# Counting a change of tile shape in the list schedule that orders a hybrid encoder's mixer

## The chip, the cores and the metric

The kernel runs on one core of one Trainium2 chip. The metric is the device time of one execution in microseconds (us). The kernel before was timed three times: 1622.95, 1623.58 and 1627.89 us, with a median of 1623.58 us. One execution was profiled; its own time is 1624.16 us, and its span from the first to the last instruction is 1622.4 us.

## The reference

Two layers work on 512 tokens of width 1024, all in float32. The change lies in the mixer of layer 0, which feeds two branches from one input projection and joins them in one output projection:

```
z   = rmsnorm(h, mix_norm) @ mix_w_in                 # 1024 -> 1792 (RWKV) + 1536 (Hyena)
y_a = rwkv7_bidir(z[..., :RWKV_COLS], ...)            # 8 heads x 64, two directions, delta-rule state
y_b = hyena_bidir(z[..., RWKV_COLS:], ...)            # gated short conv, long filter by FFT, gate
h   = h + concat([y_a, y_b]) @ mix_w_out
...
# rwkv7_bidir, one scan per direction:
sa = S kk_t ;  S = S * w_t - sa (kk_t a_t)^T + v_t k_t^T ;  y_t = S r_t
# hyena_bidir:
y = irfft(rfft(v * x1) * rfft(filter)) + (v * x1) * bias ;  y = y * x0
```

What follows in the kernel (a gated feed-forward block and a per-layer embedding in each layer, and neighbourhood attention in layer 1) is not touched by the change.

## The kernel before

The tokens lie along the free axis (512), the channels on the partitions in tiles of 128. A projection is computed as three products of rounded parts (high times high, high times low, low times high), each a TensorE matmul of 128x128 weights on 128x512 data.

`mixer0` does not write its instructions directly. `both_mixers` records every operation in a `Plan`, in groups; consecutive TensorE operations of a group are joined to a `Step` until the step's estimated cost passes 0.4. `Plan.schedule` then makes the order by list scheduling: for each engine it looks at the steps that are ready, takes those that could begin within `AHEAD` of the earliest, and of these the one of highest rank; of the five engines' candidates the earliest goes next. The rank of a step is the longest path behind it plus 1000 times the group's number in the table `ORDER`. `in_order` pins the result, so that each engine (and SP, whose queue issues all DMAs) runs its instructions in exactly that order. An instruction that waits therefore holds up all that stands behind it on its engine.

The groups, with m = 0 to 3 for four tiles of 128 channels (two heads each):

- `z,m` and `hyena,m` are input projections (72 matmuls each); `prep,m,d` makes the scan's operands for one direction d, with 64x128 products, transposes, and stores to DRAM.
- `inverse,m` inverts the triangular systems of tile m. It stores four blocks (`nd`), loads them in another layout (`w<-nd`), does 15 substitution steps on VectorE, stores and reloads (`xd`), and ends with 64x64 and 32x32 products; `kt_d` is then loaded over the inverted operand.
- `scan,m` is the recurrence over 8 chunks, each a chain of small products (64 rows or columns of the array) with copies on ScalarE and VectorE between them. `out,m` normalises its result: a product with a constant (`b<-w,con`), row sums (`b<-con,w 128x2`), a power on GpSimd, four transposes (`b<-con,w 128x128`), and the gate (`b<-sg,gup`).
- The FFT filter of Hyena: `filters` makes the filter, `fparts,j` loads it from DRAM (`w<-hw_d`), `kf,fc,j` transforms it, `signals` and `ab,fc` transform the signal (tables `wr<-in_dft_f`), `spectrum` (inside `ab`) multiplies, and `back,m` transforms back (tables `in_dft_i`, products 128x256). A table passes through a load into `wr` (3 buffers), a ScalarE rounding and a GpSimd copy into `wp`, and then a product `b<-w,wp`.
- `emb,l` projects the per-layer inputs (fills TensorE and is stored for later); `early,g` multiplies the first three finished RWKV tiles with their rows of the output weights.

In the stage's last part `scan,3`, `out,3`, `early` and `back` run; the first matmul behind the stage (line 599, tile `g`) starts at 508.26 us. All TensorE instructions recorded in a plan bear line 562 in the profile, so groups are told apart by their tiles: `b<-uv`, `b<-x,uv`, `b<-r,w` and `b<-uv,dg` are a scan, `b<-w 64x64` and `32x32` an inverse, `b<-w,wp` a transform or an embedding, `b<-xh,w` and `b<-xl,w` `early`, `b<-w 128x256` `back`.

Of the kernel before, what the change touches and what calls it, by code (L numbers as in the profile page):

```python
# [19 lines left out]
P = 128  # L20
# [184 lines left out]
class Step:  # L205

    __slots__ = ("engine", "calls", "cost", "port", "table", "bytes", "columns", "touch", "after", "then", "rank",
                 "group", "n", "left", "at", "end", "opens")

    def __init__(self, engine, group, n):  # L210
        self.engine, self.group, self.n = engine, group, n
        self.calls, self.cost, self.port, self.table, self.bytes, self.columns = [], 0.0, False, None, 0, 0
        self.touch, self.after, self.then, self.rank = {}, {}, [], 0.0
        self.opens = []


class Recorder:
# [9 lines left out]
class Plan:  # L227
# [1 line left out]

    HOP, OWN, AHEAD = 0.2, 0.1, 0.2
    DRAG, SMALL = 0.0, 5

    def __init__(self, nc):
        self.nc = nc
# [87 lines left out]
    def price(self, s, method, kw, outs, ins):  # L324

        n, e = self.width(outs[0]), s.engine
        if e == "tensor":
            rows, cols = min(P, self.rows(ins[0])), self.width(ins[0])
            if method == "transpose":
                t = n * 0.00085  # L330
            elif ins[0].dtype == F32R:
                t = 0.004 + n * 0.000447
            elif rows <= 64 or cols <= 64:
                k = (32 if rows <= 32 else 64 if rows <= 64 else P) * (32 if cols <= 32 else 64 if cols <= 64 else P)
                t = max(n * k / P / P / 500, 0.031 if cols <= 32 else 0.057)
                if cols < 4:
                    t = 0.223
            else:
                t = max(n / 600, 0.223)
            s.cost += t  # L340
            s.columns += t * 2400 * rows / P
            return
        big = sum(self.width(x) >= n for x in ins)
        if method == "memset":
            s.cost = 0.11
        elif e == "gpsimd":
            if kw.get("op") == ALU.pow:
                s.cost = 0.17 + n * 0.185
            else:
                s.cost, s.port = 0.15 + n * (0.0021 if len(ins) > 1 else 0.0009), True  # L350
        elif e == "scalar":
            s.cost = 0.16 + n * 0.00086 + 0.09 * (len(ins) - 1)
            s.table = {AF.Sin: 1, AF.Tanh: 2, AF.Exp: 2}.get(kw.get("func"))
        else:
            inner = all(x.tensor.space != PSUM for x in ins)
            if method == "tensor_reduce":
                s.cost = 0.14 + self.width(ins[0]) * 0.00105
            elif method == "tensor_tensor_scan":
                s.cost, s.port = 0.15 + n * 0.0021, True
            elif big < 2 and inner and method != "transpose":  # L360
                s.cost = 0.15 + n * 0.00053
            else:
                s.cost = 0.15 + n * 0.00106 + (0.05 if method == "scalar_tensor_tensor" else 0.0)
                s.port = inner and big > 1
# [23 lines left out]
    def schedule(self):  # L388
# [11 lines left out]
        free = dict.fromkeys(engines, 0.0)  # L400
# [3 lines left out]
        live, last, done = set(), {}, set()  # L404
# [4 lines left out]
        def key(t):  # L409
            return self.tiles[t].cap_key  # L410
# [9 lines left out]
        def start(s):  # L420

            e = s.engine
            t = max(free[e], s.at)
            want = {}
            for x in s.touch:
                if x not in live and self.pooled(x):
                    k = key(x)
                    want[k] = want.get(k, 0) + 1
            if want and (s.group not in begun or self.scarce in want):
                n = want.get(self.scarce, 0)  # L430
                g = s.group
                mine = self.reserve(g, live, [x for x in s.touch if x not in live]) if g in self.spans else 0
                rest = sum(v for h, v in reserved.items() if h != g)
                if g not in begun and not lifted and mine + n > self.SMALL:
                    n += max((self.reserve(h, live, ()) for h, r in waiting.items() if h != g and r > s.rank), default=0)
                if mine + rest + n > len(slots[self.scarce]):
                    return math.inf
            for k, n in want.items():
                have = slots[k]
                if len(have) < n:  # L440
                    return math.inf
                t = max(t, sorted(have)[n - 1])
            if s.port:
                for u, v in taken[other[e]]:
                    if u <= t < v:
                        t = v
            return t

        lifted = False
        while True:  # L450
            best = None
            waiting = {}
            for e in engines:
                for s in ready[e]:
                    g = s.group
                    if g not in begun and g in self.spans and s is self.firsts[g]:
                        waiting[g] = s.rank
            for e in engines:
                c = [(start(s), s) for s in ready[e]]
                c = [x for x in c if x[0] < math.inf]  # L460
                if not c:
                    continue
                m = max(free[e], min(x[0] for x in c)) + self.AHEAD
                t, s = max((x for x in c if x[0] <= m), key=lambda x: x[1].rank)
                if best is None or t < best[0]:
                    best = t, s
            if best is None:
                if lifted:
                    break
                lifted = True  # L470
                continue
            lifted = False
            t, s = best
            e, c = s.engine, s.cost
            ready[e].remove(s)
            if e == "tensor":
                tick = int(t / self.TICK)
                columns[tick] = columns.get(tick, 0) + s.columns
                if columns.get(tick - 1, 0) < self.COLUMNS:
                    c *= 2  # L480
            if s.table and s.table != table:
                table, c = s.table, c + 1.3
            if s.port:
                taken[e].append((t, t + c))
            free[e] = end = t + c
            if s.bytes:
                dma = max(dma, t) + s.bytes / 340e3
                end = dma + 2.1
            s.end = end
            order.append((t, s))  # L490
            g, changed = s.group, False
            for x in s.touch:
                if self.pooled(x):
                    k = key(x)
                    if x not in live:
                        live.add(x)
                        begun.add(g)
                        changed = True
                        have = slots[k]
                        have.sort()  # L500
                        have.pop(0)
                    last[x] = max(last.get(x, 0.0), end)
                    uses[x] -= 1
                    if not uses[x]:
                        slots[k].append(last[x])
                        done.add(x)
                        changed = True
            if changed and g in self.spans and g in begun:
                reserved[g] = self.reserve(g, live, (), done)
            for x in s.then:  # L510
                x.left -= 1
                x.at = max(x.at, end + (self.HOP if x.engine != e or s.bytes else self.OWN))
                if not x.left:
                    ready[x.engine].append(x)
# [50 lines left out]
class Kern:  # L565
# [186 lines left out]
    def mixer0(self):  # L752
# [17 lines left out]
        with ExitStack() as st:  # L770
# [25 lines left out]

    SLABS, PARTS = 44, 12

    ORDER = dict(start=200, low=190, filters=77, scan=100, inverse=90, prep=80, z=79, out=60, hyena=50,
                 fparts=56, kf=39, signals=62, ab=44, back=59, early=30, emb=10)  # L800

    def order(self, group):
        name, *n = group if isinstance(group, tuple) else (group,)
# [4 lines left out]
        if name in ("prep", "z"):  # L808
            n = [5 * n[0]]
        return self.ORDER[name] - (n[0] if n else 0)  # L810

# [1078 lines left out]
```

## Time and profile before

| what | value |
|---|---|
| runs | 1622.95, 1623.58, 1627.89 us (median 1623.58) |
| profiled execution: time / span | 1624.16 / 1622.4 us |
| TensorE (PE) busy over the span | 1544.8 us, 95% |
| VectorE, ScalarE, GpSimd busy | 978.7, 719.5, 325.4 us |
| stage of the mixer, until its last wait ends | 0 to 508.26 us |
| mean granted TensorE clock | 0.976 |

In the views, PE is TensorE, PEld its weight loads, DVE VectorE, ACT ScalarE, POOL GpSimd, SP (or SPq) the engine that issues DMAs. A row of windows gives, for a stretch of the span, its length, each engine's busy time in us with its number of instructions, the granted TensorE clock as a share of full speed, the DMA share and GB/s. A row of the timeline gives start, length, engine, line, operation, tiles, for a matmul the tile shape (rows by columns of the array), the count, and in brackets the idle time before it with what ended it. A float32 product shows as two matmul records, one of rounded parts and a transpose as one. A row of the chain gives start, length and what the end of the kernel waited for at that time.

### The profile page before, as it was taken

How to read it: one execution, taken by the hardware profiler on the slowest of the kernel's cores; microseconds unless marked ns; L12 is line 12 of the kernel's file. 1: busy time of each engine (PE TensorE's matmuls, PEld its weight loads, DVE VectorE, ACT ScalarE, POOL GpSimd, SP SyncE). 2: the span in 40 equal slices, each digit the busy share in tenths (PEclk: the TensorE clock that was granted, in tenths of full speed). 3: DMA queues.
4: the chain of work that ended last, by engine and by line, in shares of the span. 5: the costliest groups of instructions: out<-in, count | busy, mean ns of one | idle time of the engine just before them, and what ended most of it. 6: DMA issues, size and time to landing. Idle time of an engine off the chain costs nothing.

```text
span 1622.4 us, 24675 instructions
## 1 busy us (share of the span) xinstructions
PE 1544.8 (95%) x9576; PEld 1227.8 (76%) x9576; DVE 978.7 (60%) x1609; ACT 719.5 (44%) x1206; POOL 325.4 (20%) x286
## 2 busy tenths in 40 slices
PE   8999999996886999999999999999999999999998
PEld 6767777764565888888888878778778888888886
DVE  2587585865553766624774664565675665366654
ACT  4553635663432544413443563655554443144332
POOL 3574445533240300000001322011030000000020
PEclk9999999997987999999999999999999999999999
DMA  6366456677454233232324232323112322222421
GB/s 215 96 190 181 133 154 177 214 220 215 145 179 141 100 100 104 91 101 95 95 100 144 90 130 91 111 81 126 61 65 92 104 93 102 91 87 95 166 94 65
DMA packets 116310, 200.16 MB, mean 123 GB/s; under 512 B 27729, under 2 KB 57297, under 8 KB 116194
## 3 DMA queue, kind: packets, MB, share of 16 engines
q1 hardware_dynamic: 116194, 198.59, 38.3%
q8 instruction: 75, 1.23, 0.3%
q14 instruction: 41, 0.34, 0.1%
HBM read 166.04 MB, written 30.93 MB: 121 GB/s over the span
## 4 chain that ended last, share of the span: by engine, by line
PE 85%; DMA 4%; DVE 4%; ACT 2%; SPq 2%; POOL 1%; issue 1%; DVEq 0%; POOLq 0%; ACTq 0%
PE g L599 62%; PE b L562 19%; DVE w L562 3%; SPq L562 2%; PE m L599 1%; PE s L599 1%; DMA wr<-in_dft_f 1%; PE m L1835 1%; POOL w L562 1%; DMA wr<-in_dft_i 1%; ACT w L562 1%; ACT oh L613 0%; DMA pj_d<-w 0%; DMA wr<-in_mix_w_in 0%; DVE ol L605 0%
## 5 line engine op out<-in xcount | busy, mean ns | idle before, releaser
L605 DVE TENSOR_TENSOR wlo<-wraw,whi 128x1024 fp32r<-128x1024 f32 x186 | 235.5, 1268 | 325.8 <-ACT whi L613 321.0
L613 ACT CAST whi<-wraw 128x1024 fp32r<-128x1024 f32 x186 | 193.5, 1041 | 424.4 <-PE g L599 408.1
L599 PE MATMUL g<-xh,whi 128*128 128x512 f32 x872 | 342.0, 392 | 13.2 <-ACT whi L613 13.2
L599 PE MATMUL g<-xh,wlo 128*128 128x512 f32 x872 | 340.6, 391 | 0.0
L599 PE MATMUL g<-xl,whi 128*128 128x512 f32 x872 | 340.3, 390 | 0.0
L599 PEld LDWEIGHTS g<-xh,whi 128*128 128x128 f32 x872 | 164.4, 188 | 48.5 <-ACT whi L613 13.4
L599 PEld LDWEIGHTS g<-xh,wlo 128*128 128x128 f32 x872 | 164.2, 188 | 35.3 <-DVE wlo L605 0.8
L599 PEld LDWEIGHTS g<-xl,whi 128*128 128x128 f32 x872 | 164.3, 188 | 33.9
L605 POOL TENSOR_TENSOR nacc<-nsq 128x512 f32<-128x512 f32 x5 | 9.2, 1833 | 777.3 <-PE g L599 639.7
L562 PE MATMUL b<-xh,wp 128*128 128x512 f32 x416 | 142.2, 416 | 9.1 <-ACT wp L562 9.1
L599 PE MATMUL g<-hh,whi 128*128 128x512 f32 x352 | 137.2, 390 | 0.0
L599 PE MATMUL g<-hh,wlo 128*128 128x512 f32 x352 | 137.0, 389 | 0.0
L599 PE MATMUL g<-hl,whi 128*128 128x512 f32 x352 | 137.0, 389 | 0.0
L602 DVE SCALAR_TENSOR_TENSOR c<-u,prm,c 128x511 f32<-128x511 f32 x176 | 126.5, 747 | 6.4 <-ACT c L608 5.9
L562 PEld LDWEIGHTS b<-xh,wp 128*128 128x128 f32 x416 | 77.8, 192 | 32.6 <-ACT wp L562 10.5
L608 ACT ACTIVATE c<-u,prm 128x512 f32<-128x512 f32 x88 | 70.3, 816 | 70.8 <-DVE u L605 70.8
L562 POOL TENSOR_TENSOR wp<-wr,wp 128x512 fp32r<-128x512 f32 x60 | 80.1, 1350 | 64.9 <-ACT wp L562 30.2
L562 PE MATMUL b<-w 64*64 64x128 f32 (+5 forms) x1692 | 84.3, 253 | 7.3 <-POOL w L562 3.5
L562 POOL TENSOR_TENSOR w<-w 128x256 f32<-128x256 f32 (+2 forms) x72 | 76.6, 1083 | 68.0 <-ACT w L562 41.4
L562 PE MATMUL b<-xl,wp 128*128 128x512 f32 x208 | 85.2, 417 | 0.0
L562 PEld LDWEIGHTS b<-w 64*64 64x64 f32 (+4 forms) x1692 | 62.9, 136 | 26.5 <-issue 9.2
L605 DVE TENSOR_TENSOR u<-g,rstd 128x512 f32<-128x512 f32 x104 | 71.4, 687 | 16.5 <-PE g L599 15.6
(170 smaller groups left out, 2563.4 us busy)
## 6 DMA issues: line engine op xcount, KB each, us to landing
wraw<-in_up SPq DMA_DIRECT2D x88, 512.0 KB, 3.4
wraw<-in_down SPq DMA_DIRECT2D x44, 512.0 KB, 3.5
wr<-in_mix_w_in SPq DMA_DIRECT2D x52, 256.0 KB, 2.9
wraw<-in_na_w_qkv SPq DMA_DIRECT2D x24, 512.0 KB, 3.5
x<-ch_d SPq DMA_DIRECT2D x16, 640.0 KB, 7.2
ch_d<-w SPq DMA_DIRECT2D x64, 128.0 KB, 2.0
wraw<-in_gate SPq DMA_DIRECT2D x16, 512.0 KB, 3.5
tab<-in_rpb SPq DMA_DIRECT2D x8, 768.0 KB, 4.2
```

Of the source, the lines that this page charges most:

```text
L562: getattr(e, method)(*args, **kw)
L599: return self.nc.tensor.matmul(out, lhsT, rhs, start=start, stop=stop, skip_group_check=not group)
L602: return self.nc.vector.scalar_tensor_tensor(out=out, in0=in0, scalar=scalar, in1=in1, op0=op0, op1=op1)
L605: return (eng or self.nc.vector).tensor_tensor(out=out, in0=in0, in1=in1, op=op)
L608: return self.nc.scalar.activation(out=out, in_=in_, func=func, **kw)
L613: self.nc.scalar.copy(h, src)
L1835: nc.tensor.transpose(pst[:, i], sc[:, i // 2, (i % 2) * P:(i % 2 + 1) * P], ident)
```

## The change

Three things are edited. First, each TensorE step now carries the shape of the array that it uses (rows and columns, each 32, 64 or 128). `SWITCH` = 0.17 is added to a step's cost where its shape differs from the one before, within the step and between steps; and until a shape has run for `RUN` = 1.5, the choice on TensorE is narrowed to ready steps of the same shape, if there are any. Second, `AHEAD` goes from 0.2 to 0.15. Third, the table `ORDER` changes: the filter's transforms (`kf` 39 to 48), the signal's (`ab` 44 to 58) and `early` (30 to 48) rise, while `fparts` (56 to 40), `back` (59 to 46), `z` and `filters` (each by 2) fall. Three new entries name no group. (The attribute `opens` was not read; `issue` is written and not read.)

```
     __slots__ = (... "group", "n", "left", "at", "end", "issue", "form", "last")
...
-    HOP, OWN, AHEAD = 0.2, 0.1, 0.2
+    HOP, OWN, AHEAD = 0.2, 0.1, 0.15
     DRAG, SMALL = 0.0, 5
+
+    SWITCH, RUN = 0.17, 1.5
...  # in price(), for TensorE
+            form = tuple(32 if x <= 32 else 64 if x <= 64 else P for x in (rows, cols))
+            if s.form is None:
+                s.form = form
+            elif form != s.last:
+                t += self.SWITCH
+            s.last = form
             s.cost += t
...  # in schedule()
-        lifted = False
+        lifted, form, run = False, None, 0.0
...
-                t, s = max((x for x in c if x[0] <= m), key=lambda x: x[1].rank)
+                c = [x for x in c if x[0] <= m]
+                if e == "tensor" and run < self.RUN:
+                    c = [x for x in c if x[1].form == form] or c
+                t, s = max(c, key=lambda x: x[1].rank)
...
+                if s.form != form:
+                    run = 0.0
+                    c += self.SWITCH
+                form, run = s.last, (run if s.form == s.last else 0.0) + s.cost
...
-            free[e] = end = t + c
+            s.issue, free[e] = t, t + c
+            end = t + c
...
-    ORDER = dict(start=200, low=190, filters=77, scan=100, inverse=90, prep=80, z=79, out=60, hyena=50,
-                 fparts=56, kf=39, signals=62, ab=44, back=59, early=30, emb=10)
+    ORDER = dict(start=200, low=190, filters=75, scan=100, inverse=90, prep=80, z=77, out=60, hyena=50,
+                 fparts=40, kf=48, signals=62, ab=58, back=46, early=48, emb=10, consts=78, mid=95, last=99)
```

Both orders hold the same 2794 matmuls in the stage. The tile shape changes 275 times in the order before and 245 times in the new one. (In the new file the recorded operations bear line 578, and those behind the stage line 615.) Three places show what moved.

On TensorE, from the end of `scan,2` to the first product of `inverse,3`, before (the first row is the scan's last, the last row the inverse's first; `b<-w,wp` are the transforms `kf`):

```order
L562 MATMUL b<-x,uv 64x64 x4
L562 MATMUL b<-w,wp 128x512 x8
L562 MATMUL b<-w,con 128x512
L562 MATMUL b<-sg,gup 128x512
L562 MATMUL b<-w,wp 128x512 x6
L562 MATMUL b<-con,w 128x2 x4
L562 MATMUL b<-w,wp 128x512 x10
L562 MATMUL b<-con,w 128x128 x4
L562 MATMUL b<-w 64x64 x16
```

The same place now (`b<-con,w 128x128 x8` are the transposes of `signals`, the `b<-w,wp` belong to `emb,1`):

```order
L578 MATMUL b<-x,uv 64x64 x4
L578 MATMUL b<-w,wp 128x512 x2
L578 MATMUL b<-con,w 128x128 x8
L578 MATMUL b<-w,wp 128x512 x2
L578 MATMUL b<-w,con 128x512
L578 MATMUL b<-sg,gup 128x512
L578 MATMUL b<-w,wp 128x512 x6
L578 MATMUL b<-con,w 128x2 x2
L578 MATMUL b<-w 64x64 x32
```

All four `kf` transforms (48 matmuls) now stand further ahead, among the products of `scan,2`. Counted from the last 64x128 product of `prep,3` to the first product of `inverse,3`, there were 104 matmuls (30 of them `b<-w,wp`); now there are 282: 134 of 128x512 in rounded parts, 120 of the scan, 24 transposes, two float32 128x512 and two row sums. In the same way `inverse,1` stood behind all of `scan,0` and now stands among its products.

On SP, around the load of `inverse,3`'s blocks (`w<-nd_81`), before (`hw_d` feeds `fparts,1`; `in_dft_f` are the tables of `kf`, `pj_d` a store of `emb`):

```order
L562 DMA w<-nd_81 32x16x16 x4
L562 DMA w<-hw_d_107 128x512
L562 DMA w<-hw_d_108 128x512
L562 DMA w<-hw_d_109 128x512
L562 DMA w<-hw_d_110 128x512
L562 DMA w<-hw_d_111 128x512
L562 DMA w<-hw_d_112 128x512
L562 DMA w<-hw_d_113 128x512
L562 DMA wr<-in_dft_f 128x512
L562 DMA pj_d_128<-w 128x512
L562 DMA wr<-in_dft_f 128x512
```

And now:

```order
L578 DMA wr<-in_dft_f 128x512 x2
L578 DMA x_d_73<-w 128x512
L578 DMA pj_d_114<-w 128x512
L578 DMA pj_d_115<-w 128x512
L578 DMA wr<-in_dft_f 128x512
L578 DMA pj_d_116<-w 128x512
L578 DMA wr<-in_pT 128x512
L578 DMA s_d_77<-w 128x512
L578 DMA pj_d_117<-w 128x512
L578 DMA pj_d_118<-w 128x512
L578 DMA wr<-in_pT 128x512
L578 DMA wr<-in_proj 128x512
```

The next row is the load `w<-nd_81`. The first two tables of `kf` are now loaded ahead of the inverse's blocks, where before they stood behind them and behind seven loads of the filter.

On TensorE, from the last product of `scan,3` on, before (`b<-xh,w` and `b<-xl,w` are `early`):

```order
L562 MATMUL b<-x,uv 64x64 x4
L562 MATMUL b<-xh_371,w 128x512
L562 MATMUL b<-xh_521,w 128x512
L562 MATMUL b<-xh_371,w 128x512
L562 MATMUL b<-xh_521,w 128x512
L562 MATMUL b<-xl_522,w 128x512
L562 MATMUL b<-xh_521,w 128x512
L562 MATMUL b<-xl_522,w 128x512
L562 MATMUL b<-xh_521,w 128x512
L562 MATMUL b<-xl_522,w 128x512
L562 MATMUL b<-xh_521,w 128x512
L562 MATMUL b<-w,con 128x512
```

And now, up to the end of the stage (`b<-w 128x256` is `back`):

```order
L578 MATMUL b<-x,uv 64x64 x4
L578 MATMUL b<-w 128x256 x16
L578 MATMUL b<-w,con 128x512
L578 MATMUL b<-sg,gup 128x512
L578 MATMUL b<-w 128x256 x8
L578 MATMUL b<-con,w 128x2 x4
L578 MATMUL b<-w 128x256 x24
L578 MATMUL b<-con,w 128x128 x4
L578 MATMUL b<-w 128x256 x32
L615 MATMUL g<-xh_1150,whi 128x512
```

Before, 60 matmuls of `early`, all 96 of `back` and `out,3` followed the scan's last product. Now `early` and 16 matmuls of `back` stand within `scan,3`, and 80 of `back` with `out,3` behind it.

More of the change, by code (lines that the diff above doesn't have):

```diff
@@ L207 @@
     __slots__ = ("engine", "calls", "cost", "port", "table", "bytes", "columns", "touch", "after", "then", "rank",
-                 "group", "n", "left", "at", "end", "opens")
+                 "group", "n", "left", "at", "end", "issue", "form", "last")
     def __init__(self, engine, group, n):
@@ L213, in __init__ @@
         self.touch, self.after, self.then, self.rank = {}, {}, [], 0.0
-        self.opens = []
+        self.form = self.last = None
 class Recorder:
```

## The prediction

> **What bounds the kernel now.** I read the page first, then the windows of its stages.
>
> ```profile
> span 1622.4 us, 24675 instructions
> PE 1544.8 (95%) x9576; PEld 1227.8 (76%) x9576; DVE 978.7 (60%) x1609; ACT 719.5 (44%) x1206; POOL 325.4 (20%) x286
> PE   8999999996886999999999999999999999999998
> PEclk9999999997987999999999999999999999999999
> ```
>
> TensorE is the bound. Its only weak slices are the tenth to the thirteenth, 365 to 527 us, where the granted clock falls too. Windows cut the stage at four events: the last product of `prep,3`, the first of `inverse,3`, and both ends of `scan,3`.
>
> ```profile
> core 0: us, PE busy (x) PEld busy (x) DVE busy (x) ACT busy (x) POOL busy (x), PEclk, DMA share, GB/s
> 0.00:360.70 360.70, 344.43 (x3431) 258.36 (x3432) 240.17 (x450) 192.25 (x397) 183.69 (x189) 0.99 0.58 175
> 360.70:394.20 33.50, 16.78 (x131) 11.61 (x129) 16.91 (x48) 11.66 (x26) 10.53 (x10) 0.69 0.71 201
> 394.20:414.10 19.90, 14.91 (x283) 10.85 (x282) 13.02 (x22) 7.44 (x19) 4.68 (x5) 0.94 0.81 240
> 414.10:455.40 41.30, 37.48 (x428) 26.09 (x427) 28.07 (x45) 17.07 (x48) 18.31 (x15) 0.87 0.41 130
> 455.40:508.30 52.90, 33.77 (x173) 27.82 (x173) 21.04 (x33) 14.50 (x24) 13.29 (x12) 0.85 0.54 182
> 507.50:1622.40 1114.90, 1097.50 (x5136) 893.07 (x5136) 659.57 (x1015) 477.30 (x695) 94.87 (x56) 0.99 0.30 99
> ```
>
> Behind the stage TensorE idles 17.4 us in 1114.9 and the change touches nothing there, so 1114.9 us stand. In the stage it idles 508.3 - 447.4 = 60.9 us, 44.6 of them behind 360.7. The timeline names the idle times in brackets, and the SP rows what the queue did meanwhile.
>
> ```profile
> 363.13 1.76 SPq L562 DMA_DIRECT2D nd<-w  x3
> 369.17 2.20 SPq L562 DMA_DIRECT2D w<-nd  x4
> 371.48 3.27 SPq L562 DMA_DIRECT2D w<-hw_d  x7
> 374.80 0.42 SPq L562 DMA_DIRECT2D wr<-in_dft_f  x1
> 381.52 3.78 PE L562 MATMUL b<-w,wp 128*128 128x512 f32 x8 [13.53 <-ACT wp L562]
> 394.21 1.15 PE L562 MATMUL b<-w 64*64 64x64 f32 x32
> 402.33 4.44 SPq L562 DMA_DIRECT2D w<-kt_d  x4
> 406.87 8.92 SPq L562 DMA_DIRECT2D wr<-in_dft_f  x5
> 412.98 1.22 PE L562 MATMUL b<-w,wp 128*128 128x512 f32 x2 [4.99 <-ACT wp L562]
> 470.99 2.12 PE L562 MATMUL b<-xh,w 128*128 128x512 f32 x8 [3.09 <-POOL w L562]
> 508.26 0.79 PE L599 MATMUL g<-xh,whi 128*128 128x512 f32 x1 [13.18 <-ACT whi L613]
> ```
>
> When `scan,2` ends, at 368 us, `inverse,3` is still between its stores (363.13) and its products (394.21), 31.1 us of copies and substitution. The only other work, `kf`, waits 13.53 us for a table that SP issues at 374.80, behind `w<-nd` and seven `hw_d` loads. At 408 us the second pair of tables costs 4.99 us more.
>
> **The change part by part.** The sum is made against the profiled execution, 1624.16 us, which is 0.58 above the median of the runs; 1.76 us of it lie outside the span.
>
> *The wait at 368.* The order now puts 282 matmuls between the last product of `prep,3` and the first of `inverse,3`, of which 134 take 128x512. The next rows give 0.23 us from one of these to the next: 30.8 us, against the 31.1 us between store and product, with 120 scan products and 24 transposes besides. All `kf` stand in it, and their first tables stand ahead of `w<-nd` on SP. The cover is there: -13.5 us. Bounds: 0 if the wait reappears whole elsewhere, -13.5.
>
> ```profile
> 191.77 0.45 PE L562 MATMUL b<-x,uv 128*64 128x64 f32 x8
> 192.05 0.40 PE L562 MATMUL b<-uv,w 128*64 128x64 f32 x8
> 194.64 0.39 PE L562 MATMUL b<-xh,wp 128*128 128x512 f32 x1
> 194.87 0.39 PE L562 MATMUL b<-xl,wp 128*128 128x512 f32 x1
> 195.10 0.40 PE L562 MATMUL b<-xh,wp 128*128 128x512 f32 x1
> 195.43 0.45 PE L562 MATMUL b<-uv,x 128*64 128x64 f32 x8
> 195.81 0.50 PE L562 MATMUL b<-xh,wp 128*128 128x512 f32 x1
> ```
>
> *Changes of shape.* Starts are 0.23 us apart within a shape (194.87 to 195.10) and 0.33 where the shape changes (195.10 to 195.43). Leaving the narrow shape takes 0.38 (195.43 to 195.81) against 0.28 within it (191.77 to 192.05). A change costs 0.10 us. The order has 275 before and 245 now, so 30 x 0.10 = -3.0 us, all on TensorE's own path. Bounds: 0, if the saved changes stood beside waits, and 30 x 0.15 = -4.5, the 0.38 less a dense step's 0.23. The planner's price of 0.17 is only a rank and is not a time. The Trainium skill sees it dearer: "TensorEngine Tiling", Key Properties, says that a change of tiling mode drains the engine, and "TensorE: Matmul & The Clock Gate", Single matmul latency, puts the part of a matmul that does not stream at about 166 ns warm. By that the term would be -5.0 and the total 2 us lower; the rows say 0.10.
>
> *The wait at 408.* The tables of `kf` no longer lie there. But `inverse,3` must still hand over: `kt_d` is loaded over its operand (issued from 402.33, all four by 406.77) before the scan's first product. The nearest row for that join without a table is `inverse,2`, whose scan then waits:
>
> ```profile
> 322.75 0.66 PE L562 MATMUL b<-con,w 128*128 128x128 f32 x4
> 324.40 1.45 PE L562 MATMUL b<-w 64*128 64x512 f32 x4 [0.53 <-ACT w L562]
> 328.75 0.45 PE L562 MATMUL b<-x,uv 64*64 64x64 f32 x8 [2.14 <-ACT w L562]
> ```
>
> Waits of 0.53 and 2.14 us. Now only six 128x512 products (1.4 us) stand between the inverse's last and the scan's first product. I leave 2.5 us of wait there, so -2.5. Bounds 0 and -5.0.
>
> *The clock.* Windows on the stretches of half clock show what the waits cost afterwards.
>
> ```profile
> 329.60:336.50 6.90, 6.90 (x68) 4.52 (x67) 3.78 (x6) 5.08 (x13) 2.75 (x4) 0.51 0.76 265
> 367.20:387.70 20.50, 6.88 (x21) 4.37 (x21) 10.53 (x35) 3.14 (x7) 2.96 (x3) 0.50 0.72 209
> 411.60:418.40 6.80, 5.42 (x38) 3.61 (x38) 0.00 (x0) 2.08 (x5) 1.23 (x2) 0.50 0.46 152
> sum 58.40, PE 35.73 PEld 26.15 DVE 26.89 ACT 13.93 POOL 11.62; mean PE 5.10 PEld 3.74 DVE 3.84 ACT 1.99 POOL 1.66
> ```
>
> The sum is over all seven such stretches to 507.5: PE busy for 35.73 us at half clock, half of it lost, 17.9 us. Those behind the two waits that go hold 6.88 + 5.42 = 12.3, so -6.2 us. Bounds: 0 (new waits of like size) and -17.9. The row at 329.60 follows waits of 0.53 and 2.14 us only, so I expect the short waits that stay at the joins to keep the rest. The Trainium skill has another rule: "TensorE: Matmul & The Clock Gate", HAM oscillation, asks only that no gap exceed some 3.4 us. By it the short waits would cost no clock, the term would be -17.9 and the total 1590.3. The row at 329.60 does not agree, and I give that rule one chance in ten, as part of the second rival.
>
> *Behind `scan,3`.* `early` (60 matmuls) and 16 of `back` move ahead of the scan's last product. TensorE's work is only placed elsewhere, so this has no term by itself; but the cover of `out,3` gets thinner. Its steps took, from the scan's last products to the end of its transposes, 454.68 + 0.69 to 467.30 + 0.60:
>
> ```profile
> 454.68 0.69 PE L562 MATMUL b<-x,uv 128*64 128x64 f32 x6
> 467.30 0.60 PE L562 MATMUL b<-con,w 128*128 128x128 f32 x4
> L562 PE MATMUL b<-w 128*128 128x256 f32 x96 | 14.5, 310 | 2.9 <-ACT w L562 1.4 <-POOL w L562 1.4
> ```
>
> That is 12.5 us. Now 48 products of `back` lie beside it before its transposes, 48 x 14.5/96 = 7.2 us, and its own ten matmuls, some 2.3 us (four transposes 0.6, the others by their neighbours' 0.2 to 0.6). So 3.0 us of new wait: +3.0. Bounds 0 and +12.5. The 13.18 us at the end stay: they are the last copies, SP's loads and a weight tile, as before.
>
> *Costed at nothing.* DMA and instruction counts are the same but for two more table loads on ACT, early in the filter. Each takes 1.28 us beside an ACT that is busy 192 of 360.7 us; 0, at most +2.6.
>
> ```profile
> L562 ACT ACT_TABLE_LOAD x5 | 6.4, 1283 | 4.0 <-DMA w<-in_xT 4.0
> ```
>
> `AHEAD` only breaks ties by rank. The 3.09 us at 468, where `early,1` waits for POOL, could go, since other work stands there, or grow, since POOL still splits `ab,1`'s spectrum before those weights: 0, bounds -3.1 and +5. The projections `hyena` slide later into `scan,0` and `scan,1`, under a TensorE that already idles only 16.3 of 360.7 us: 0.
>
> Sum: -13.5 - 3.0 - 2.5 - 6.2 + 3.0 = -22.2; 1624.2 - 22.2 = **1602.0 us**. All lower bounds together give -44, all upper ones +20; neither is likely, since a wait that stays also keeps its clock.
>
> **The rivals.**
>
> *The idle time moves.* Spectrum copies on POOL (18.3 us busy in 41.3 during `scan,3`) or the tables hold TensorE where the new order puts their products. For it: 470.99 shows such a wait now, and `early` stands closer behind `ab,1`. Against: `kf` no longer shares those engines. If half of the gain returns, 1624.2 - 11 = 1613; the span 1608 to 1619 belongs to it.
>
> *More goes than two waits.* Of the 60.9 us idle in the stage, 60.9 - 13.5 - 5.0 - 3.1 - 13.2 = 26.1 lie in shorter pieces and at the start, and some of the pieces are followed by lost clock. With more transforms within `scan,2`, and `ab,1`, `early` and a part of `back` within `scan,3`, a third of these (8) and half of the remaining clock loss (11.7/2) could go: 1602 - 14 = 1588.
>
> *Nothing but the shapes.* TensorE's total does not fall beyond 3.0 us if the chain `prep`, `inverse`, `scan`, `out` sets the end: 1621, the same within 0.3%. I count 0.3% (4.9 us) as what a measurement of this kernel can tell from no change. Against: that chain was slack by 13.5 + 5.0 us in the rows above.
>
> *Slower.* One mechanism: products of a transform wait within a scan for a table that SP has not issued, and all scan products behind them wait too, since TensorE keeps its order. The two pairs of `kf` tables cost 13.53 + 4.99 = 18.5, or 9.3 us a pair. Six pairs now lie in or before a scan's products (`kf`, `ab`, `back`); to lose 4.9 us against before, 22.2 + 4.9 = 27.1 us must come back, that is three pairs. With four it would be 1602 + 37 = 1639. It decides as soon as SP reaches those loads behind a blocked store. For it: SP's rows at 371.48. Against: the two first tables now stand ahead of `w<-nd`.
>
> **How the numbers follow.** Forecast (1594 to 1608) 0.53; idle time moves (1608 to 1619) 0.16; more goes (below 1594) 0.14; nothing but the shapes 0.07; slower 0.10. The likeliest gives 1602. Faster by over 0.3% is the first three, 0.83; same 0.07; slower 0.10. Range: at the low end 1586, leaving 0.05; at the high end 1619, leaving 0.15. Nearly all of the chance lies on one side, so one range serves.
>
> **What would show it.** Right: the stage's last wait before line 599 ends near 486 us (508.3 - 22); no wait for `wp` above 3 us between `scan,2` and `scan,3`; half clock within the stage at under 24 us of PE busy; from the end of `scan,3` to line 599 about 30 us in place of 52.9; a change of shape still 0.10 us. Wrong: brackets `<-ACT wp` or `<-POOL w` of several us within the scans, or a first `inverse` product that comes over 31 us after its stores with TensorE idle.

## The result, and the profile after

The changed kernel takes 1609.93 us (median of five runs, 1605.59 to 1614.65) against 1623.58 us before (five runs, 1622.95 to 1628.55): a ratio of 0.9906, 95% interval 0.9879 to 0.9934. The gain of 13.7 us is real, but it is three fifths of the 22.2 us that were forecast. The profiled execution took 1609.93 us, its span is 1608.1 us. The lines of the page that answer to those of before:

```profile
span 1608.1 us, 24664 instructions
PE 1532.4 (95%) x9576; PEld 1220.4 (76%) x9576; DVE 971.2 (60%) x1609; ACT 720.3 (45%) x1208; POOL 325.8 (20%) x286
PE   8989989889896999999999999999999999999997
PEclk9999999999898999999999999999999999999999
```

The weak slices, the tenth to the thirteenth, read 9896 where they read 6886, and four of the first nine have gone from 9 to 8. The windows, cut at the same five events of the order as before (the columns are those of the prediction's windows; the last row has the length of the last row there and begins 2.9 us ahead of the stage's end, in a wait of TensorE), say how much:

```profile
0.00:341.40 341.40, 310.45 (x3203) 233.73 (x3204) 220.59 (x436) 177.34 (x363) 176.13 (x183) 0.99 0.57 167
341.40:393.20 51.80, 47.35 (x361) 34.27 (x359) 31.93 (x68) 26.82 (x59) 21.11 (x20) 0.97 0.70 214
393.20:413.70 20.50, 17.78 (x303) 13.75 (x303) 14.51 (x24) 9.18 (x22) 6.41 (x6) 1.00 0.95 299
413.70:467.80 54.10, 48.12 (x481) 35.70 (x481) 32.48 (x51) 23.33 (x59) 24.44 (x20) 0.91 0.56 183
467.80:496.10 28.30, 13.26 (x99) 11.62 (x97) 12.00 (x20) 7.22 (x12) 2.82 (x3) 0.82 0.53 185
493.20:1608.10 1114.90, 1095.43 (x5136) 891.33 (x5136) 659.75 (x1015) 477.46 (x695) 94.88 (x56) 0.99 0.31 100
```

From the last product of `prep,3` to the first of `inverse,3` TensorE now idles 51.80 - 47.35 = 4.5 us, where it idled 16.7. But ahead of it, to 341.4, it idles 341.40 - 310.45 = 31.0 us, where it idled 16.3 to 360.7. Over the whole stage it idles 59.1 us (the first five rows) against 60.9. The timeline shows the form in which the idle time came back (rows of TensorE):

```profile
88.32 0.50 PE L578 MATMUL b<-xh,wp 128*128 128x512 f32 x1 [2.78 <-ACT wp L578]
149.78 2.08 PE L578 MATMUL b<-w 64*64 64x64 f32 x64 [2.02 <-DVE w L578]
214.28 0.45 PE L578 MATMUL b<-r,w 64*64 64x64 f32 x8 [2.29 <-ACT r L578]
307.06 0.74 PE L578 MATMUL b<-xh,wp 128*128 128x512 f32 x2 [2.51 <-issue]
352.64 0.45 PE L578 MATMUL b<-uv,w 128*64 128x64 f32 x8 [2.03 <-ACT w L578]
370.54 1.20 PE L578 MATMUL b<-w,wp 128*128 128x512 f32 x4 [0.94 <-ACT wp L578]
393.23 2.25 PE L578 MATMUL b<-w 64*64 64x64 f32 x64
413.74 1.17 PE L578 MATMUL b<-uv,w 128*64 128x64 f32 x8 [2.47 <-DMA w<-kt_d]
477.51 4.03 PE L578 MATMUL b<-w 128*128 128x256 f32 x32
496.09 0.80 PE L615 MATMUL g<-xh,whi 128*128 128x512 f32 x1 [14.54 <-ACT whi L629]
```

No wait inside the stage is longer than 2.78 us, apart from the 7 us at its start that both kernels have; the 14.54 us end it. Waits of 0.4 to 3.2 us there are 30, together 34.0 us, against 20 with 19.7 us before, counted over all rows of both stages. Two of the five stretches of half clock in the stage, and the sum over all five:

```profile
226.70:233.50 6.80, 5.82 (x40) 4.36 (x40) 1.41 (x2) 4.58 (x11) 0.00 (x0) 0.50 0.31 70
414.40:421.30 6.90, 6.33 (x57) 4.75 (x58) 2.79 (x6) 2.79 (x8) 0.61 (x1) 0.51 0.72 219
sum 30.40, PE 18.84 PEld 14.46 DVE 8.20 ACT 11.74 POOL 1.29; mean PE 3.77 PEld 2.89 DVE 1.64 ACT 2.35 POOL 0.26
```

The spans differ by 14.3 us. Of this, idle time in the stage gives 1.8 (60.9 - 59.1), half clock 8.4 ((35.73 - 18.84)/2), the rest of TensorE's busy time in the stage 2.0 (447.4 - 436.9 - 8.4, rounded), and the part behind the stage 2.1 (508.26 and 496.09 taken from the spans; no instruction changed there). This says where the time went, not why. It also rests on one execution of each kernel: the five executions of the changed kernel have granted clocks of 0.981 to 0.987, and the profiled one is at the top of them, so its share for the clock may be high.

### The profile page after: what moved, and what is told of

Read it like the earlier page. It is cut to its first block, busy times and chain, and to the rows that moved or that the text cites. A ratio compares the mean times of both kernels' runs of the same rounds, so it can differ in the third digit from the quotient of the medians.

```text
span 1608.1 us, 24664 instructions
## 1 busy us (share of the span) xinstructions
PE 1532.4 (95%) x9576; PEld 1220.4 (76%) x9576; DVE 971.2 (60%) x1609; ACT 720.3 (45%) x1208; POOL 325.8 (20%) x286
## 4 chain that ended last, share of the span: by engine, by line
PE 80%; DMA 6%; DVE 5%; ACT 3%; SPq 2%; issue 2%; POOL 1%; POOLq 0%; ACTq 0%; DVEq 0%
PE g L615 62%; PE b L578 14%; DVE w L578 4%; SPq L578 2%; DMA wr<-in_mix_w_in 2%; PE s L615 1%; PE m L615 1%; DMA wr<-in_dft_f 1%; DMA w<-kt_d 1%; ACT w L578 1%; PE m L1851 1%; DMA wr<-in_dft_i 0%; ACT oh L629 0%; DVE ol L621 0%; DMA wraw<-in_mix_w_out_b 0%
## 5 line engine op out<-in xcount | busy, mean ns | idle before, releaser
L615 PE MATMUL g<-xh,whi 128*128 128x512 f32 x872 | 341.7, 392 | 14.5 <-ACT whi L629 14.5
L578 PE MATMUL b<-w 64*64 64x128 f32 (+5 forms) x1692 | 77.4, 245 | 7.3 <-DVE w L578 3.1
L578 DVE TENSOR_TENSOR w<-w 128x512 f32<-128x512 f32 (+16 forms) x120 | 72.4, 624 | 11.6 <-DMA w<-hw_d 4.4
```

What stands on the lines that cost most here:

```text
L578: getattr(e, method)(*args, **kw)
L615: return self.nc.tensor.matmul(out, lhsT, rhs, start=start, stop=stop, skip_group_check=not group)
```

## The experiments

All were timed in three rounds beside the kernel before, whose medians on that chip were 1627.69 us (e1 to e4), 1625.22 us (e5 to e8) and 1627.77 us (the last four). Ratios are to it, with 95% intervals.

**Which part of the change brings the gain.** The kernel before with the new table alone:

```
 # before.py
-    ORDER = dict(start=200, low=190, filters=77, ...
+    ORDER = dict(start=200, low=190, filters=75, ...      # all rows of the new table
```

> The scheduler of before with the new ORDER table alone (AHEAD 0.2, no cost of a shape, no narrowing). The order has 266 changes of shape, 9 fewer than before. Theory A, the table carries the gain: all four kf have their first tables ahead and 88 matmuls of 128x512 stand between the last product of prep,3 and the first of inverse,3, so the waits of 13.5 and 5.0 us and the half clock behind them go, and the run comes out near the new kernel, 1608 to 1616 us. Theory B, the rule on shapes carries the gain: 9 x 0.10 = 0.9 us, 1621 to 1625 us. Short waits of 0.4 to 3.2 us (19.7 us before, 34.0 us in the new kernel): A expects 25 or more if the table makes them, B about 20.

Measured: 1660.06 us, ratio 1.0206 (1.0153 to 1.0259). The new scheduler with the old table:

```
 # after.py
-    ORDER = dict(start=200, low=190, filters=75, ...
+    ORDER = dict(start=200, low=190, filters=77, ...      # the old table
```

> The new scheduler (SWITCH 0.17, RUN 1.5, AHEAD 0.15) with the old ORDER table. 234 changes of shape, 41 fewer than before: -4.1 us by 0.10 each. Theory A (the table carries the gain): 1616 to 1625 us, the waits of before move but stay. Theory B (the rule carries it): 1606 to 1614 us. If the narrowing makes the short waits of the new kernel, they rise here too (above 28 us); if the table makes them, they stay near 20.

Measured: 1632.22 us, ratio 1.0025 (0.9996 to 1.0054). Neither part brings anything alone, and both theories missed both times. The rule alone saves 41 changes of shape (234 for 275) and the stage still ends 12.6 us later in its profile. The changed kernel with two numbers of the table put back:

```
 # after.py
-    ORDER = dict(..., filters=75, ..., z=77, ...
+    ORDER = dict(..., filters=77, ..., z=79, ...
```

> The new kernel with two numbers of ORDER put back (z 79, filters 77). 235 changes of shape. Theory A1, the lower rank of the input projections makes the short waits ahead of scan,2: they fall by about half of the added 14 us and the time by as much, 1600 to 1605 us. Theory A2, the short waits come with any order that fills the long ones, because each product then stands closer behind its operand: no gain, 1607 to 1615 us.

Measured: 1624.21 us, ratio 0.9987 (0.9961 to 1.0013): two numbers take the gain away, which neither theory had. The kernel before with only the other rows of the table changed:

```
 # before.py
-    ORDER = dict(..., fparts=56, kf=39, ..., ab=44, back=59, early=30, ...)
+    ORDER = dict(..., fparts=40, kf=48, ..., ab=58, back=46, early=48, ...)
```

> The scheduler of before with only the late rows of the new table (kf 48, ab 58, early 48, back 46, fparts 40; z and filters old). 266 changes of shape. Up to prep,3 the order stays that of before, so the short waits there should stay as before. Theory A1: only the late waits go and nothing is given back early: 1603 to 1609 us. Theory A2: the order behind scan,2 only exchanges its long waits for short ones and for the clock: 1611 to 1618 us. Theory B (rule): 1621 to 1625 us.

Measured: 1644.43 us, ratio 1.0095 (1.0064 to 1.0126), outside all three theories. Its profile has a new wait of 14.47 us from 460 on, for GpSimd among the products of `early`:

```profile
474.69 1.65 PE L562 MATMUL b<-xh,w 128*128 128x512 f32 x3 [14.47 <-POOL w L562]
```

That is the wait which the rival "the idle time moves" named, not the late table of the slower rival.

**Whether TensorE's work is what bounds the stage.** With the order pinned, 80 of the dense products of `emb` are left out (all but the first of each sum, so the embeddings are incomplete):

```
 # where a step is issued, in before.py and in after.py
+            thin = s.engine == "tensor" and isinstance(s.group, tuple) and s.group[0] == "emb"
             for method, args, kw in s.calls:
+                if thin:
+                    if not kw["start"]:
+                        continue
+                    kw = dict(kw, stop=True)
                 getattr(e, method)(*args, **kw)
```

> The order of before, kept step by step, but each product of the embeddings (emb) issues only the first of its six matmuls: 80 of the 888 matmuls of 128x512 in the stage are left out, all other instructions stand (the embeddings are then wrong by what is left out). At 0.234 us each that is 18.7 us of TensorE work. 40 of them lay in the stretch from scan,1 to scan,2, where TensorE idled 1.0 us of 75.6. Theory C, these matmuls are cover for the latency of the scans and inverses: the time falls by less, since waits appear where they stood, 8 to 14 us. Theory W, TensorE's work sets the time and waits are separate: -18.7 us.

> The same in the order of the new kernel: 80 matmuls of emb left out, 18.7 us of work. There all of emb stands between the products of scan,2 and up to inverse,3, as the cover that the new order moved there. Theory C: waits come back in that stretch (idle there was 9.8 us), and the time falls by 4 to 11 us, less than in the order of before. Theory W: -18.7 us, as in before.

Measured: in the order before 1626.62 us, ratio 1.0004 (0.9975 to 1.0033); in the new order 1608.97 us, ratio 0.9906 (0.9873 to 0.9939), the changed kernel's own ratio. The windows on their stages, the first up to line 604 of e5_thin_before and the second up to line 620 of e6_thin_new (these lines are 599 and 615 of the unthinned files):

```profile
0.00:516.10 516.10, 441.78 (x4361) 328.37 (x4361) 319.38 (x595) 243.24 (x512) 230.73 (x230) 0.92 0.58 173
```

```profile
0.00:495.35 495.35, 426.11 (x4360) 319.16 (x4360) 311.21 (x595) 243.83 (x514) 231.01 (x230) 0.95 0.60 181
```

80 x 0.234 = 18.7 us of TensorE's work are gone from each, and neither kernel is faster. Theory W is out; theory C expected a fall of 8 to 14 us in the order before, which did not come either. In the new order busy time fell by 10.8 us (436.95 to 426.11) and idle time grew by 10.1 (59.1 to 69.2); the rest went into half clock, which covers 36.7 us of busy time in place of 18.84. In the order before the profile is of the slowest of ten executions, 5.2 us above their median, and its stage is 7.8 us longer: idle time grew by 13.4 us (60.9 to 74.3), and half clock covers 59.2 us of busy time in place of 35.73, another 11.7 us.

So TensorE's work is not the bound of this stage, in which it is busy for 88% of the time (95% is its share of the whole span): the dense products taken out were cover, work that fills the time while the next step of the chain `prep`, `inverse`, `scan`, `out` is not ready, and what is taken from it comes back as waiting and, in the two profiles nearly as much, as half clock. This fits the waits that moved and did not go: the amount of cover is fixed, and the new order takes it mostly from the first scans (128x512 products in rounded parts from the first product of `scan,0` to the first of `scan,2`: 316 before, 222 now) to put it into `scan,2` (68 before, 210 now).

**The wait at 368 by itself.** The order before, where only four table loads of SP move: two of `kf` ahead of the load of `inverse,3`'s blocks and two behind it, all ahead of the seven `hw_d`:

```
 # before.py, behind plan.schedule()
+            nd = [i for i, s in enumerate(order) if s.engine == "sync" and s.group == ("inverse", 3)
+                  and s.calls[0][2]["in_"].tensor.name == self.nd[3].tensor.name]
+            for fc, at in ((1, nd[-1] + 1), (0, nd[0])):
+                early = [s for s in order if s.engine == "sync" and s.group == ("kf", fc, 0)]
+                for s in early:
+                    order.remove(s)
+                order[at:at] = early
```

> The order of before on every engine, with one thing moved: on SP the two table loads of kf,0,0 stand ahead of the loads w<-nd of inverse,3, and the two of kf,1,0 behind them, ahead of the seven loads w<-hw_d, so they are issued some 5 us sooner. If SP's order made the wait of 13.53 us at 368, it shrinks to 6 to 9 us, and the half clock behind it by 1 to 3 us: 5 to 8 us in all. If the inverse's own chain sets the pace there, only the wait moves: kf ends sooner, TensorE waits the same time before the inverse's first product, and the time stays within 2 us.

Measured: 1625.36 us, ratio 1.0008 (0.9980 to 1.0037). Rows of its timeline, SP and TensorE:

```profile
369.87 1.76 SPq L562 DMA_DIRECT2D nd<-w  x3
375.61 1.08 SPq L562 DMA_DIRECT2D wr<-in_dft_f  x2
376.80 2.10 SPq L562 DMA_DIRECT2D w<-nd  x4
```

```profile
379.87 2.08 PE L562 MATMUL b<-w,wp 128*128 128x512 f32 x4 [4.90 <-ACT wp L562]
383.60 2.08 PE L562 MATMUL b<-w,wp 128*128 128x512 f32 x4 [1.65 <-ACT wp L562]
390.83 2.08 PE L562 MATMUL b<-w,con 128*128 128x512 f32 x2 [5.16 <-DVE w L562]
401.59 1.15 PE L562 MATMUL b<-w 64*64 64x64 f32 x32
```

The first table is now issued 0.6 us behind the end of `scan,2` (374.97), where it was 6.8 us (367.99 and 374.80). The waits for tables shrink from 13.53 us to 4.90 + 1.65 = 6.55, but a wait for VectorE of 5.16 comes up, 11.7 us in all. From the stores of `nd` to the first product of the inverse it takes 31.7 us (369.87 to 401.59), where it took 31.1: the inverse's own chain sets the pace here, as the second theory had it. What the bracket named was the last to be late, not the reason why TensorE had nothing to do.

**How much the rule's numbers bear.** The changed kernel without the narrowing, then with `AHEAD` back, then with a lower price of a change:

```
 # after.py, e8
-    SWITCH, RUN = 0.17, 1.5
+    SWITCH, RUN = 0.17, 0.0
 # after.py, e9
-    HOP, OWN, AHEAD = 0.2, 0.1, 0.15
+    HOP, OWN, AHEAD = 0.2, 0.1, 0.2
 # after.py, e10
-    SWITCH, RUN = 0.17, 1.5
+    SWITCH, RUN = 0.1, 1.5
```

> The new kernel with RUN = 0: a change of shape still costs 0.17 in the plan, but the choice is not narrowed to the running shape. 292 changes of shape, 47 more than in the new kernel: +4.7 us by 0.10 each. Its order has 362, 44, 70, 122 and 94 matmuls of 128x512 from the start, from scan,0, scan,1, scan,2 and scan,3 on, and 196 left behind the last product of scan,3 (none in the new kernel). Theory C (cover): the scans' stretches idle and the 196 come on top, 1640 to 1670 us. Theory W: about 1615 us.

> The changed kernel with one number of its rule moved, AHEAD from 0.15 to 0.2; the table stays. 234 changes of shape instead of 245, and 24 dense products remain behind the last product of `scan,3` where the changed kernel has none. Theory S (the numbers of table and rule fit one schedule, and a small move of any of them loses most of the gain): 1616 to 1630 us, as in e3_z_filters_back. Theory R (the rule brings a gain over a breadth of its numbers, and e3 was a bad draw): within 4 us of the changed kernel's 1609.9, and by fewer changes (11 x 0.10) 1 us below it.

> The changed kernel with the price that its scheduler puts on a change of shape moved from 0.17 to 0.10 us, which is what the rows of before show for one; the table stays. 24 dense products remain behind the last product of `scan,3`. Theory S (table and rule fit one schedule): 1616 to 1630 us. Theory R (the gain has breadth): within 4 us of 1609.9.

Measured: e8 1632.68 us, ratio 1.0049 (1.0018 to 1.0080); e9 1634.29 us, ratio 1.0046 (1.0022 to 1.0070); e10 1653.25 us, ratio 1.0174 (1.0132 to 1.0216). Theory R falls, theory S was still too mild, and e8 lies between its two theories: each of the three moves costs the whole gain and more, also where the shape changes less often than in the changed kernel (e9: 234 times for 245). What these orders share with e1 and e2 is a wait of 15.5 to 26.6 us ahead of `back` that neither of the two kernels has. Rows of e9_ahead_02, three engines, from the last transform to the first product of `back`:

```profile
450.21 6.91 PE L578 MATMUL b<-w,wp 128*128 128x512 f32 x22
459.51 8.41 DVE L578 TENSOR_TENSOR w<-w 128x512 f32<-128x512 f32 x13
465.64 9.50 POOL L578 TENSOR_TENSOR w<-w 128x512 fp32r<-128x512 f32 x6 [5.50 <-ACT w L578]
473.96 7.15 DVE L578 TENSOR_TENSOR w<-w 128x512 f32<-128x512 f32 x10 [6.04 <-POOL w L578]
483.61 0.58 PE L578 MATMUL b<-w 128*128 128x256 f32 x1 [26.49 <-ACT w L578]
513.09 0.79 PE L615 MATMUL g<-xh,whi 128*128 128x512 f32 x1 [12.15 <-ACT whi L629]
```

This is the second chain of the stage: the last transform of `ab,1`, its spectrum on VectorE and GpSimd, `back`, and the next weights. It takes 513.09 - 457.12 = 56.0 us, and for 26.5 of them TensorE waits ahead of `back`. The table reads both chains in each trace: the end of the last `b<-w,wp`, the end of `scan,3`, and the start of the first matmul behind the stage (us). Each row is one execution, up to 9 us off the median of its kernel (e4), so only large differences count.

| kernel | last transform | `scan,3` ends | stage ends | behind the transform | behind the scan |
|---|---|---|---|---|---|
| before | 436.2 | 455.4 | 508.3 | 72.1 | 52.9 |
| after | 435.9 | 467.8 | 496.1 | 60.2 | 28.3 |
| e1 (table alone) | 486.4 | 461.8 | 541.9 | 55.5 | 80.1 |
| e2 (rule alone) | 467.4 | 465.3 | 520.9 | 53.5 | 55.6 |
| e3 (two numbers back) | 456.6 | 457.0 | 508.2 | 51.6 | 51.2 |
| e4 (other rows alone) | 442.0 | 454.0 | 521.5 | 79.5 | 67.5 |
| e5 (thin, order before) | 446.7 | 465.7 | 516.1 | 69.4 | 50.4 |
| e6 (thin, new order) | 439.4 | 471.3 | 495.4 | 56.0 | 24.1 |
| e7 (tables first) | 441.7 | 460.9 | 511.9 | 70.2 | 51.0 |
| e8 (no narrowing) | 473.6 | 419.9 | 520.0 | 46.4 | 100.1 |
| e9 (`AHEAD` 0.2) | 457.1 | 440.2 | 513.1 | 56.0 | 72.9 |
| e10 (`SWITCH` 0.1) | 485.4 | 464.7 | 543.1 | 57.7 | 78.4 |

In no run did the stage end sooner than 24 to 28 us behind `scan,3` (e6, after), or sooner than 46 to 58 us behind the last transform (e1, e2, e3, e6, e8, e9, e10). These are the shortest distances seen; that they are limits is not shown. The changed kernel is close to both at once. Every order that lost the gain (e4 apart) has its transforms 20 to 50 us later, and in all of these but e3 the wait for the spectrum then holds the end: in e8 `scan,3` is done at 419.9, 48 us ahead of the changed kernel, to no avail. Before, neither chain was near its shortest; behind `scan,3` TensorE itself still had 33.8 us of `early`, `out,3` and `back` to do. So the gain in the two profiled spans is read in one line: 24.6 us less behind `scan,3`, 12.4 us more ahead of it, 2.1 us behind the stage, together 14.3.

**The price of a change of shape.** At the end of the kernel before stand 200 dense and 400 narrow products whose results nothing reads, once in turns (two and four) and once grouped:

```
+        if grouped:
+            for _ in range(100):
+                dense()      # two 128x512 products
+            for _ in range(100):
+                narrow()     # four 64x64 products
+        else:
+            for _ in range(100):
+                dense()
+                narrow()
```

> The kernel of before with work put in at its end, whose results nothing reads: 100 times two dense products of 128x512 and four products of 64x64, alternating, so 199 changes of shape more. Taken together with p2_grouped, where the same 600 products stand as 200 dense and then 400 narrow (1 change). If a change costs what the two rows of before show (0.10 us), this run is 198 x 0.10 = 19.8 us longer than p2_grouped. If it costs the scheduler's 0.17 us, 33.7 us longer. If it costs nothing of its own, the two are level within 3 us.

> The same work as p1_alternating, grouped: 200 dense products, then 400 narrow ones, one change. The added work alone: 200 x 0.234 us of dense products and 400 narrow ones at some 0.06 to 0.07 us each, 47 + 24 to 28 = 71 to 75 us above the kernel of before if each product keeps the duration of its row. By 0.10 us per change p1_alternating ends 19.8 us later than this run, by 0.17 us 33.7 us later, by nothing within 3 us.

Measured: 1725.82 and 1691.68 us, ratios 1.0622 (1.0584 to 1.0659) and 1.0409 (1.0369 to 1.0448). The difference of 34.1 us over 198 changes is 0.17 us for one, about 0.13 to 0.22 by the two intervals. In the traces it is (103.96 - 68.98)/198 = 0.177. A window over the added work of p1_alternating, and a piece of its timeline:

```profile
1613.09:1717.05 103.96, 103.96 (x1001) 60.79 (x999) 4.53 (x8) 0.83 (x2) 0.00 (x0) 1.00 0.03 11
```

```profile
1640.02 0.73 PE L599 MATMUL m<-xh 128*128 128x512 f32 x2
1640.68 0.45 PE L599 MATMUL m<-con 64*64 64x64 f32 x8
1641.06 0.73 PE L599 MATMUL m<-xh 128*128 128x512 f32 x2
1641.72 0.45 PE L599 MATMUL m<-con 64*64 64x64 f32 x8
```

and the added work of p2_grouped in its timeline, 45.43 us to the change and 23.55 behind it:

```profile
1618.84 45.49 PE L599 MATMUL m<-xh 128*128 128x512 f32 x200
1664.27 23.55 PE L599 MATMUL m<-con 64*64 64x64 f32 x800
```

In turns, two dense products take 0.66 us (1640.02 to 1640.68) where grouped ones take 0.45, and four narrow ones 0.38 (1640.68 to 1641.06) where grouped ones take 0.24. The two changes of a turn thus cost 0.35 us. Each shows in two spacings, and the prediction read only the one at the change. The other stood in the profile of before, one row ahead of those quoted:

```profile
194.30 0.50 PE L562 MATMUL b<-xl,wp 128*128 128x512 f32 x1
```

From this product, the first behind a scan's, to the next dense one at 194.64 are 0.34 us, where 0.23 were taken to be the step within a shape. Over the stage of before, at full clock, the median of some 80 such spacings is 0.337 us, that of some 620 spacings between dense products that follow a dense one 0.233. The Trainium skill's rule that the prediction set aside, "TensorEngine Tiling", Key Properties, with "TensorE: Matmul & The Clock Gate", Single matmul latency (some 166 ns), agrees with the 0.17 to 0.18 measured. That a drain is the cause no run here shows.

## Why the prediction was right and where it was wrong

The direction and the range (1586 to 1619) hold; the likeliest time, 1602.0, is 7.9 us too low, and 1609.9 lies where the rival "the idle time moves" was put (1608 to 1619), just outside the forecast's own part (1594 to 1608). That the direction came true is in part luck: the term that carried the forecast, the waits, gave 1.8 us of 13.0, and most of the gain is half clock, of which 6.2 were forecast, and a part behind the stage of which nothing was. (The 0.15 left above 1619 are also less than the 0.07 and 0.10 of the two rivals put there, 0.17.) By the prediction's steps:

- *The wait at 368, -13.5.* The step that failed. Locally it came true: no wait for `wp` above 0.94 us between `scan,2` and `scan,3`, and `inverse,3` is covered. "The cover is there" counted the products now standing in that place and not those missing where they had stood. Up to the last product of `prep,3` idle time grew by 14.7 us, and over the stage all waits together gave 1.8 us instead of the net 13.0 of the three wait terms (-13.5, -2.5, +3.0). e5 to e7 show that less of TensorE's work, or an earlier table, does not shorten the stage; that waits therefore move with the cover is the reason that fits, and it was not tested by itself.
- *The wait at 408, -2.5.* 4.99 us became the 2.47 us of `kt_d`: as forecast, to 0.1 us.
- *Changes of shape, -3.0.* The price was wrong, 0.17 to 0.18 and not 0.10, and so was the remark that the planner's 0.17 is no time. It decided nothing: by 0.175, 30 changes are 5.3 us, and TensorE's busy time apart from the clock fell by 2.0. e2 saves 41 changes and gains nothing. In the traces that time does not even follow the count: e8 has 292 changes and 425.4 us busy without the clock's part, the changed kernel 245 and 427.5. How much of a saved change a stage returns as waiting was not separated.
- *The clock, -6.2.* It gave 8.4. Half-clock work is 18.84 us, below the 24 named. That it can come with short waits holds again: the stretch at 226.7 begins behind a wait of 1.38 us and within one of 1.33 us (those ahead of 225.27 and 227.69 in the timeline). Waits of 2.29 to 2.78 us (ahead of 88.32, 214.28 and 307.06) are followed by none, so the length of one wait does not tell. The rule of the Trainium skill on gaps of some 3.4 us ("TensorE: Matmul & The Clock Gate", HAM oscillation) does not agree with this trace either.
- *Behind `scan,3`, +3.0.* Too dear: of the 15.0 us that TensorE idles there, 14.5 are the wait at the end. Only 0.5 lie beside `out,3`, and the end wait grew by 1.4. From the end of the scan to line 615 it takes 28.3 us; about 30 were forecast.
- *When the stage ends.* 486 was forecast, 496.1 came. The 30 us behind the scan were right, so the miss lies ahead of it: `scan,3` should have ended at 456 and ended at 467.8.
- *Costed at nothing.* The 3.09 us of `early,1` went, inside its bounds. Of the 2.1 us behind the stage, 1.0 is half clock that the wait at the end leaves behind (5.70 us of busy time before, 3.67 now, halved); the rest has no cause in the change that the record shows: that part takes 1112.1 to 1114.7 us in the profiles of e1 to e4, with the same instructions.
- *The rivals.* The idle time moved, but by another mechanism than the spectrum copies and tables that were named. "Nothing but the shapes" was set aside because its chain "was slack by 13.5 + 5.0 us": that argument is wrong, since TensorE waiting does not make the chain slack; in e7 the chain through `inverse,3` keeps its 31 us though the tables come earlier. Slower is what the table alone is, but not by the late tables that the rival named: e1 has a wait for `wp` of 5.13 us at 473, behind its scans, and then 26.42 us for the spectrum.

Two things stay open. Why the new order's first part waits 14.7 us more was not tested with cover put back there alone; that cover left it is counted, and that less cover turns into waiting and half clock is shown by e6. And the changed kernel is the only one of the eight orders tried with the new rule or table that gains, so nothing here says that the rule is better than the one before in general.

## What to carry to other kernels

A high busy share (95% over this kernel, 88% in the stage that changed) does not make an engine the bound: read the share in the stage, leave out some of its work with the order pinned, and if the time stays, that work is cover, and removing one long wait may only move it. Where work is reordered, count the cover at the place it leaves as well as where it goes, and read each chain's distance to the end of the stage; the gain here was what the later one of them allowed. A schedule found by numbers in a table is one schedule: measure neighbours of it before crediting the rule.

## What the runs showed of the hardware that was not expected

A change of the array's shape between 128x512 products in rounded parts and 64x64 float32 products costs 0.17 to 0.18 us (the mean of both directions), spread over the spacing at the change and the one behind it (a dense product between narrow ones has 0.33 us to the next narrow one or 0.34 to the next dense one, for 0.23), so that a single spacing shows only a part of it. The granted clock fell to half for 6.8 us behind a wait of 1.38 us and within one of 1.33, and did not fall behind single waits of 2.29 to 2.78 us.
